# Order of the MLA up-projection and the stick-breaking value projection in a hybrid decoder trunk

## The chip, the cores and the metric

The kernel runs on one core of one Trainium2 chip. The metric is the device time of one execution in microseconds. Before the change the median of three runs is 1052.58 us, from 1045.85 to 1053.77 us.

A core has engines that run side by side, each with an instruction queue of its own: TensorE (PE in the profile; PEld is its weight load), VectorE (DVE), ScalarE (ACT), GpSimd (POOL), and SyncE (SP), which here issues transfers. An engine takes its queue in order. The order of a queue is laid down when the kernel is compiled: the order in which the Python code emits instructions is a priority, and an instruction that the compiler takes to be ready may be put ahead of one emitted earlier that is not.

## The reference, cut to what matters

Two layers; each is half a SwiGLU block, a mixing block, and half a SwiGLU block, on 256 tokens of width 1024, in float32. In the mixing block one projection `h @ w_in` feeds three groups of heads:

```python
(c_q, c_kv, k_rope, n_q, n_kc, n_vc, n_ks, n_vs, n_kw, n_vw, n_gate,
 sb_q, sb_k, sb_v) = jnp.split(h @ w_in[l], split_at, axis=-1)
o_mla = mla_attention(c_q, c_kv, k_rope, ...)       # 6 heads; q and k/v come from low-rank latents
o_nsa = nsa_attention(...)                          # 6 heads, sparse
o_sb = stick_breaking_attention(sb_q, sb_k, sb_v)   # 4 heads, no softmax
x = x + concat([o_mla, o_nsa, o_sb]) @ w_out[l]
```

MLA (latent attention) normalises the latents `c_q` (256 wide) and `c_kv` (128 wide), multiplies them by up-projections `w_uq` and `w_ukv`, and turns 32 columns of each query and of the shared key by a rotary position (rope).

## The kernel before, in words

**Matmuls.** To keep float32 accuracy each matrix is split into a high and a low part (`split`, lines 91 to 98: ACT writes the high part `wh`, DVE subtracts to get the low part `wl`), and each product takes three matmuls. Weights arrive in `raw` tiles (4 buffers); `wh` and `wl` have 5 buffers each, so a weight piece can be split only when the matmuls of an older piece are done. PSUM tiles are banks by tag (`a0`, `a1`, `g0`, `g1`), two of each.

**The mixing block** is `mix` (line 825). It projects K, Q, V and gates of the sparse heads, then the latents (`C_A`), then queries and keys of stick-breaking (`C_SQ`), then its values (`C_SV`). `project` (line 389) issues two loads of `w_in` on SP, makes four split pieces, and gives 48 matmuls on two `a0` banks, which `evac` copies out. `weave` puts steps of the sparse attention (`nsa`) between the steps of a projection, as priorities. The sparse attention has 23 steps: 5 are taken with the `C_V` projection, 10 with `C_A`, and the last 8 within the first four steps of `C_SQ`, so none is left for the weaves behind.

**The steps that the change concerns.** `latents` (line 530, called at 908) transposes the latents on PE (line 537, six transposes on `g0` and `g1`) and writes `ch` on ACT (541) and `cl` on DVE (542). The `C_SV` projection (909) and its evacuation to `SV` follow, half on ACT, half on DVE. Then `up_project` (545, called at 916) loads `w_uq` and `w_ukv` on SP (547, 550), makes three split pieces (two 576 wide, one 768 wide), and for each of two token tiles gives 18 matmuls on `g0` and `g1` (12 for the queries, 288 wide, and 6 for keys and values, 384 wide), evacuates them to `qm`, `km`, `vm`, and turns the rope columns with six POOL instructions (`rope`, lines 467 to 473: two products and a sum for the queries, the same for the key).

Then come the dense attentions: `stick_breaking` (576) transposes `SQ` (583), copies it to `sT`, and needs `SV` only for its outputs (620); `latent_attention` (625) first transposes `qm` and `km` on PE (632). Both are mixed with `out_sparse` (954), the part of the output projection that needs only the sparse heads; it takes two `a0` banks and split pieces of `w_out`.

Of the kernel before, what the change touches and what calls it, by code (L numbers as in the profile page):

```python
# [10 lines left out]
F32 = mybir.dt.float32  # L11
# [51 lines left out]
def trunk(ctx, tc, a, out):  # L63
# [4 lines left out]
    sb = ctx.enter_context(tc.tile_pool(name="sb", bufs=1))  # L68
# [5 lines left out]
    def raw_tile():  # L74
        return sb.tile([128, 2048], F32, name="raw", tag="raw", bufs=4)
# [6 lines left out]
    def bank(tag):  # L82
        return ps.tile([128, 512], F32, name="bk" + tag, tag=tag, bufs=2)
# [4 lines left out]
    def mm(o, l, r, start, stop):  # L88
        PE.matmul(o, l, r, start=start, stop=stop, skip_group_check=True)  # L89

    def split(src, n, shape=None, **dims):
        h, lo = split_tiles(n)
        hv, lv = h, lo
        if shape:
            hv, lv = h.rearrange(shape, **dims), lo.rearrange(shape, **dims)
        ACT.activation(hv, src, AF.Copy)  # L96
        DVE.tensor_tensor(lv, src, hv.bitcast(F32), op=OP.subtract)  # L97
        return hv, lv
# [75 lines left out]
    def gam(n, l, k):  # L174
        if n == "ffn1_norm":
            return cols1[:, l * KD + k:l * KD + k + 1]
        c = gcol[n, l] + k
        return cols[:, c:c + 1]
# [210 lines left out]
    def project(l, c0, c1, tag):  # L389

        w = c1 - c0
        p = [bank(tag) for _ in range(2)]

        def step(kh, k2, raw):
            W = split(raw[:, 2 * k2:2 * k2 + 2], 2 * w, "p (k f) -> p k f", k=2)
            for j in range(2):
                k = kh * 4 + k2 * 2 + j
                for t in range(2):
                    s = slice(t * 128, t * 128 + 128)
                    o = p[t][:, :w]  # L400
                    mm(o, xh[:, k, s], W[0][:, j], k == 0, False)
                    mm(o, xh[:, k, s], W[1][:, j], False, False)
                    mm(o, xl[:, k, s], W[0][:, j], False, k == KD - 1)

        for kh in range(2):
            raw = raw_tile()[:, :4 * w].rearrange("p (k f) -> p k f", k=4)
            nc.sync.dma_start(raw, a["w_in"][l, kh * 512:(kh + 1) * 512, c0:c1].rearrange("(k p) f -> p k f", p=128))
            for k2 in range(2):
                step(kh, k2, raw)
                yield p  # L410
        yield p

    def run(g, n=100):
        last = None
        for _ in range(n):
            try:
                last = next(g)
            except StopIteration:
                break
        return last  # L420

    def weave(g, h, n):

        last = None
        for last in g:
            run(h, n)
        return last

    def chain(*gens):
        for g in gens:  # L430
            yield from g
# [13 lines left out]
    def evac(i, o, p, scale):  # L445
        if i % 2 == 0:
            ACT.activation(o, p, AF.Copy, scale=scale)
        else:
            DVE.tensor_scalar(o, p, scale, None, op0=OP.mult)
# [11 lines left out]
    def rope(x, cos, sin, half, n, o=None, no=None):  # L461
        v = x.rearrange("p h (two f) -> p h two f", two=2)
        t1 = sb.tile([128, 192], F32, name="rt1", tag="rt1", bufs=2)[:, :n * 2 * half].rearrange("p (h f) -> p h f", h=n)
        t2 = sb.tile([128, 192], F32, name="rt2", tag="rt2", bufs=2)[:, :n * 2 * half].rearrange("p (h f) -> p h f", h=n)
        c = cos.rearrange("p (o f) -> p o f", o=1).to_broadcast([128, n, 2 * half])
        s = sin.rearrange("p (o two f) -> p o two f", o=1, two=2).to_broadcast([128, n, 2, half])
        POOL.tensor_tensor(t1, x, c, op=OP.mult)  # L467
        POOL.tensor_tensor(t2.rearrange("p h (two f) -> p h two f", two=2), v[:, :, ::-1, :], s, op=OP.mult)  # L468
        if o is None:
            POOL.tensor_tensor(x, t1, t2, op=OP.add)  # L470
        else:
            b = [128, no, 2 * half]
            POOL.tensor_tensor(o, t1.to_broadcast(b), t2.to_broadcast(b), op=OP.add)
# [56 lines left out]
    def latents(l, A, ch, cl):  # L530

        for b0, nb in ((0, 2), (2, 1)):
            p = bank("g%d" % (b0 // 2))
            for b in range(nb):
                for t in range(2):
                    c = (b0 + b) * 128
                    PE.transpose(p[:, b * T + t * 128:b * T + t * 128 + 128], A[:, t, c:c + 128], ident)
            for b in range(nb):
                g = gam("mla_q_norm", l, b) if b0 == 0 else gam("mla_kv_norm", l, 0)
                pb = p[:, b * T:b * T + T]  # L540
                ACT.activation(ch[b0 + b], pb, AF.Copy, scale=g)
                DVE.scalar_tensor_tensor(cl[b0 + b], pb, g, ch[b0 + b].bitcast(F32), op0=OP.mult, op1=OP.subtract)
            yield

    def up_project(l, A, ch, cl, lr, qm, km, vm):
        raw = raw_tile()[:, :1152].rearrange("p (k f) -> p k f", k=2)
        nc.sync.dma_start(raw, a["mla_w_uq"][l].rearrange("(k p) f -> p k f", p=128))
        wuq = [split(raw[:, k], 576) for k in range(2)]
        raw = raw_tile()[:, :768]
        nc.sync.dma_start(raw, a["mla_w_ukv"][l])  # L550
        wkv = split(raw, 768)
        for t in range(2):
            s = slice(t * 128, t * 128 + 128)
            q, k = qm[t], km[t]
            for c in range(2):
                p = bank("g%d" % c)[:, :288]
                f = slice(c * 288, c * 288 + 288)
                for kk in range(2):
                    mm(p, ch[kk][:, s], wuq[kk][0][:, f], kk == 0, False)
                    mm(p, ch[kk][:, s], wuq[kk][1][:, f], False, False)  # L560
                    mm(p, cl[kk][:, s], wuq[kk][0][:, f], False, kk == 1)
                evac(c, q[:, 3 * c:3 * c + 3].rearrange("p h d -> p (h d)"), p, lr[:, t:t + 1])
            for c in range(2):
                p = bank("g%d" % c)[:, :384]
                f = slice(c * 384, c * 384 + 384)
                mm(p, ch[2][:, s], wkv[0][:, f], True, False)
                mm(p, ch[2][:, s], wkv[1][:, f], False, False)
                mm(p, cl[2][:, s], wkv[0][:, f], False, True)
                ph = p.rearrange("p (h d) -> p h d", h=3)
                evac(c, k[:, 3 * c:3 * c + 3, 0:64], ph[:, :, 0:64], lr[:, 2 + t:3 + t])  # L570
                evac(c, vm[:, t, 3 * c:3 * c + 3], ph[:, :, 64:128], lr[:, 2 + t:3 + t])
            rope(q[:, :, 64:96], cosm[:, t], sinm[:, t], 16, 6)
            rope(A[:, t:t + 1, 384:416], cosm[:, t], sinm[:, t], 16, 1, o=k[:, :, 64:96], no=6)
            yield
# [250 lines left out]
    def mix(l):  # L825
# [57 lines left out]
        nsa = chain(cmp, sparse_rows(), sparse_attention(NQ, nT, gt, vbd, pct))  # L883
# [3 lines left out]
        A = sb.tile([128, 2, 448], F32, name="A", tag="A")[:, :, :416]  # L887
# [7 lines left out]
        lr = small.tile([128, 4], F32, name="lr", tag="lr")  # L895
# [6 lines left out]
        ch, cl = [chl[0][:, 0], chl[0][:, 1], chl[2][:, 0]], [chl[1][:, 0], chl[1][:, 1], chl[2][:, 1]]  # L902
        p = weave(project(l, C_SQ, C_SV, "a0"), nsa, 2)
        SQ = sb.tile([128, 2, 512], F32, name="SQ", tag="pj")
        for t in range(2):
            evac(0, SQ[:, t, 0:256], p[t][:, 0:256], r8[:, t:t + 1])
            evac(1, SQ[:, t, 256:512], p[t][:, 256:512], r[:, t:t + 1])
        run(latents(l, A, ch, cl))
        p = weave(project(l, C_SV, C_END, "a0"), nsa, 2)
        SV = sb.tile([128, 2, 256], F32, name="SV", tag="SV")  # L910
        for t in range(2):
            evac(t, SV[:, t], p[t][:, :256], r[:, t:t + 1])
        qm = [sb.tile([128, 6, 96], F32, name="qm", tag="qm", bufs=2) for _ in range(2)]
        km = [sb.tile([128, 6, 96], F32, name="km", tag="km", bufs=2) for _ in range(2)]
        vm = sb.tile([128, 2, 6, 64], F32, name="vm", tag="vm")
        weave(up_project(l, A, ch, cl, lr, qm, km, vm), nsa, 2)
        run(nsa)
        attn = mixed(stick_breaking(SQ, SV), latent_attention(qm, km, vm))

# [105 lines left out]
    for l in range(DEPTH):  # L1025
        ffn("ffn1", l, nxt=("mix_norm", l), first=l == 0)
        mix(l)
        if l + 1 < DEPTH:
            ffn("ffn2", l, nxt=("ffn1_norm", l + 1))
        else:  # L1030
            ffn("ffn2", l, final=True)
# [25 lines left out]
```

## Time and profile before

| | us |
|---|---|
| median of 3 runs | 1052.58 (1045.85 to 1053.77) |
| the profiled execution, its own time | 1054.14 |
| its span, first to last instruction | 1052.3 |
| PE busy | 1027.7 (98%) |
| DVE busy | 699.7 (66%) |
| ACT busy | 578.1 (55%) |
| POOL busy | 76.9 (7%) |

Times in a trace are microseconds from the start of the span. Busy is time in which an engine executes; it says nothing about speed. PEclk, the granted clock, is the share of full speed at which PE was let run in a stretch: 1.00 is 2.4 GHz and 0.50 is 1.2 GHz, and values between are a mean over both. The chain that ended last goes back from the last instruction, at each step to what released it. The mixing block of layer 0 ends near 344 us, that of layer 1 near 859 us.

### The profile page before, as it was taken

What the parts mean: (1) busy time and instruction counts of PE and PEld (TensorE: products, weight loads), DVE (VectorE), ACT (ScalarE), POOL (GpSimd) and SP (SyncE); (2) the same over time, 40 slices, a digit from 0 to 9 for tenths busy, and PEclk for the clock granted to TensorE, in tenths of its full rate; (3) what the DMA queues carried; (4) which work ended last, traced back from release to release, by engine and by line L of the source; (5) the groups of instructions that cost most, each with busy time, mean ns of one, the idle gap of its engine ahead of it and who ended that gap; (6) DMA issues with size and microseconds to landing.
All of it is one profiled execution on the core that took longest, in us unless ns stands there. A gap on an engine that the chain in (4) does not pass through costs nothing.

```text
span 1052.3 us, 15114 instructions
## 1 busy us (share of the span) xinstructions
PE 1027.7 (98%) x5743; PEld 874.0 (83%) x5743; DVE 699.7 (66%) x1132; ACT 578.1 (55%) x1082; POOL 76.9 (7%) x137
## 2 busy tenths in 40 slices
PE   7999999999999999999999999999999999999996
PEld 6888888897776888888888888889877778888885
DVE  6766666766635766666676666667766567666664
ACT  5555555646546655555565555556455575555553
POOL 2000000123301000000000000002142100000001
PEclk9999999999979999999999999999999999999999
DMA  9556464571322546464546556455514334645531
GB/s 314 203 181 224 140 236 152 168 233 48 117 94 81 187 174 220 143 237 165 196 136 225 178 182 216 146 200 175 190 51 130 121 121 160 238 151 211 192 129 40
DMA packets 128405, 176.38 MB, mean 168 GB/s; under 512 B 4567, under 2 KB 107213, under 8 KB 128333
## 3 DMA queue, kind: packets, MB, share of 16 engines
q1 hardware_dynamic: 127840, 174.83, 49.0%
q8 instruction: 45, 0.74, 0.3%
q10 hardware_dynamic: 492, 0.59, 0.2%
q14 instruction: 28, 0.22, 0.1%
HBM read 174.36 MB, written 1.05 MB: 167 GB/s over the span
## 4 chain that ended last, share of the span: by engine, by line
PE 90%; DVE 3%; ACT 2%; DMA 2%; POOL 2%; issue 1%; SPq 0%; POOLq 0%; ACTq 0%
PE bkg L308 45%; PE bka L89 37%; PE bkg L89 5%; DVE wl L97 1%; DMA raw<-in_ffn_w_gate_dram 1%; PE bkg L632 1%; POOL rt L467 1%; PE bkg L202 1%; ACT wh L96 0%; POOL rt L468 0%; ACT junk L213 0%; DMA x_tok<-in_x_dram 0%; DMA raw<-in_ffn_w_up_dram 0%; ACT xhl L207 0%; DMA raw<-in_w_out_dram 0%
## 5 line engine op out<-in xcount | busy, mean ns | idle before, releaser
L97 DVE TENSOR_TENSOR wl<-raw,wh 128x1024 fp32r<-128x1024 f32 (+5 forms) x336 | 395.9, 1181 | 203.9 <-ACT wh L96 201.3
L96 ACT ACTIVATE wh<-raw 128x1024 fp32r<-128x1024 f32 (+5 forms) x336 | 340.3, 1016 | 229.4 <-PE bkg L308 174.8
L308 PE MATMUL bkg<-xhl,wh 128*128 128x512 f32 (+1 forms) x1440 | 348.9, 384 | 0.2 <-DVE xhl L208 0.2
L308 PEld LDWEIGHTS bkg<-xhl,wh 128*128 128x128 f32 x1440 | 259.3, 189 | 47.9 <-PE bkg L202 0.3
L308 PEld LDWEIGHTS bkg<-xhl,wl 128*128 128x128 f32 x1392 | 189.9, 190 | 13.1
L308 PE MATMUL bkg<-xhl,wl 128*128 128x256 f32 x1392 | 195.2, 282 | 0.0
L89 PE MATMUL bka<-wh,hh 128*128 128x512 f32 x352 | 138.8, 394 | 0.3 <-ACT hh L336 0.2
L89 PE MATMUL bka<-wl,hh 128*128 128x512 f32 x352 | 138.3, 393 | 0.0
L89 PE MATMUL bka<-wh,hl 128*128 128x512 f32 x352 | 136.7, 390 | 0.6 <-DVE hl L337 0.6
L336 ACT ACTIVATE hh<-t 128x256 fp32r<-128x256 f32 x88 | 36.8, 418 | 127.0 <-DVE t L333 127.0
L89 PE MATMUL bka<-wh,xhl 128*128 128x384 f32 (+4 forms) x384 | 106.4, 349 | 0.0
L89 PEld LDWEIGHTS bka<-wh,hl 128*128 128x128 f32 x352 | 66.1, 188 | 15.8 <-DVE hl L337 1.7
L89 PEld LDWEIGHTS bka<-wh,hh 128*128 128x128 f32 x352 | 66.4, 189 | 13.2 <-ACT hh L336 2.1
L89 PEld LDWEIGHTS bka<-wl,hh 128*128 128x128 f32 x352 | 66.4, 189 | 10.3
L89 PEld LDWEIGHTS bka<-wh,xhl 128*128 128x128 f32 x384 | 68.8, 189 | 5.7 <-issue 1.7
L89 PE MATMUL bka<-wl,xhl 128*128 128x384 f32 (+4 forms) x192 | 65.9, 343 | 0.0
L337 DVE TENSOR_TENSOR hl<-t,hh 128x256 fp32r<-128x256 f32 x88 | 37.4, 425 | 40.7 <-ACT hh L336 40.7
L222 POOL TENSOR_TENSOR r<-r,nhalf 128x2 f32<-128x2 f32 x5 | 3.5, 704 | 597.8 <-DVE r L221 597.8
L459 ACT ACTIVATE P<-bka,st 128x256 f32<-128x256 f32 (+1 forms) x72 | 29.4, 418 | 22.4 <-DVE st L763 14.2
L325 DVE TENSOR_TENSOR t<-bkg,t 128x256 f32<-128x256 f32 x88 | 36.8, 418 | 6.3 <-ACT t L324 6.3
L333 DVE TENSOR_TENSOR t<-t,t 128x256 f32<-128x256 f32 x88 | 37.4, 425 | 3.8 <-ACT t L327 0.9
L326 DVE TENSOR_TENSOR t<-t,rb 128x256 f32<-128x256 f32 x88 | 37.4, 425 | 2.8
(229 smaller groups left out, 949.4 us busy)
## 6 DMA issues: line engine op xcount, KB each, us to landing
raw<-in_ffn_w_down_dram SPq DMA_DIRECT2D x44, 1024.0 KB, 6.6
raw<-in_ffn_w_gate_dram SPq DMA_DIRECT2D x43, 1024.0 KB, 6.7
raw<-in_ffn_w_up_dram SPq DMA_DIRECT2D x43, 1024.0 KB, 5.2
raw<-in_w_in_dram SPq DMA_DIRECT2D x8, 768.0 KB, 4.8
raw<-in_w_out_dram SPq DMA_DIRECT2D x20, 256.0 KB, 4.6
raw<-in_w_in_dram SPq DMA_DIRECT2D x4, 1024.0 KB, 7.1
raw<-in_w_in_dram SPq DMA_DIRECT2D x4, 832.0 KB, 4.5
raw<-in_w_in_dram SPq DMA_DIRECT2D x4, 804.0 KB, 4.4
```

The costliest lines, as they stand in the source:

```text
L89: PE.matmul(o, l, r, start=start, stop=stop, skip_group_check=True)
L96: ACT.activation(hv, src, AF.Copy)
L97: DVE.tensor_tensor(lv, src, hv.bitcast(F32), op=OP.subtract)
L202: PE.transpose(p[:, i * T + t * 128:i * T + t * 128 + 128], x_tok[:, t, d * 128:d * 128 + 128], ident)
L308: PE.matmul(*args, **flags)
L325: DVE.tensor_tensor(gn, pg[:, :T], g2, op=OP.add)
L326: DVE.tensor_tensor(gn, gn, rb, op=OP.mult)
L333: DVE.tensor_tensor(h, gn, un, op=OP.mult)
L336: ACT.activation(hh, h, AF.Copy)
L337: DVE.tensor_tensor(hl, h, hh.bitcast(F32), op=OP.subtract)
L459: state["last_exp"] = ACT.activation(*args, **kw).ins
L467: POOL.tensor_tensor(t1, x, c, op=OP.mult)
```

## The change

The latents stay where they are in the code. The whole of `up_project` (its two loads, three split pieces, 36 matmuls, evacuations and ropes) is emitted ahead of the `C_SV` projection (its two loads, four split pieces, 48 matmuls and two evacuations) instead of behind it, in both layers. No instruction is added or removed.

```diff
@@ -906,14 +906,14 @@
         run(latents(l, A, ch, cl))
-        p = weave(project(l, C_SV, C_END, "a0"), nsa, 2)
-        SV = sb.tile([128, 2, 256], F32, name="SV", tag="SV")
-        for t in range(2):
-            evac(t, SV[:, t], p[t][:, :256], r[:, t:t + 1])
         qm = [sb.tile([128, 6, 96], F32, name="qm", tag="qm", bufs=2) for _ in range(2)]
         km = [sb.tile([128, 6, 96], F32, name="km", tag="km", bufs=2) for _ in range(2)]
         vm = sb.tile([128, 2, 6, 64], F32, name="vm", tag="vm")
         weave(up_project(l, A, ch, cl, lr, qm, km, vm), nsa, 2)
+        p = weave(project(l, C_SV, C_END, "a0"), nsa, 2)
+        SV = sb.tile([128, 2, 256], F32, name="SV", tag="SV")
+        for t in range(2):
+            evac(t, SV[:, t], p[t][:, :256], r[:, t:t + 1])
         run(nsa)
         attn = mixed(stick_breaking(SQ, SV), latent_attention(qm, km, vm))
```

## Rows read from the trace of the kernel before

**Rows 1.** The page, part 4: the chain that ended last, by engine.

```profile
PE 90%; DVE 3%; ACT 2%; DMA 2%; POOL 2%; issue 1%; SPq 0%; POOLq 0%; ACTq 0%
```

**Rows 2.** Tile qm, who waited for it: us, times (both layers).

```profile
  PEld bkg L632: 4.4, 2
  PE bkg L632: 3.9, 2
```

**Rows 3.** Chain that ended last, layer 0: start, length, what.

```profile
281.72 0.44 DVE qm L449
...
284.94 1.59 POOL rt L467
286.53 0.56 POOL rt L468
287.09 0.66 POOL rt L467
287.75 1.19 POOL rt L468
288.94 0.56 POOL qm L470
289.50 0.04 issue
289.54 1.20 PE bkg L632 x7
...
344.45 0.44 PE bkg L202 x2
```

**Rows 4.** Windows: stretch, length, busy (instructions) PE, PEld, DVE, ACT, POOL; PEclk, DMA, GB/s.

```profile
284.90:290.00 5.10, 3.17 (x21) 2.37 (x19) 4.54 (x6) 2.56 (x5) 5.10 (x7) 1.00 0.36 117
290.00:344.40 54.40, 52.71 (x251) 39.14 (x249) 26.38 (x48) 29.49 (x70) 4.13 (x7) 0.87 0.26 83
344.40:500.00 155.60, 155.55 (x847) 135.20 (x848) 107.90 (x157) 85.89 (x140) 0.71 (x1) 1.00 0.55 191
```

**Rows 5.** Windows of 4 us, same columns, both layers.

```profile
288.00:292.00 4.00, 2.46 (x13) 1.77 (x13) 2.12 (x3) 0.58 (x1) 2.04 (x3) 0.80 0.47 135
292.00:296.00 4.00, 4.00 (x11) 2.86 (x10) 0.00 (x0) 1.54 (x3) 0.00 (x0) 0.50 0.00 0
...
300.00:304.00 4.00, 4.00 (x13) 3.34 (x12) 0.68 (x2) 1.91 (x5) 0.61 (x1) 0.50 0.00 0
304.00:308.00 4.00, 4.00 (x25) 3.13 (x24) 3.66 (x7) 1.55 (x2) 0.00 (x0) 0.99 0.07 10
808.00:812.00 4.00, 2.89 (x13) 2.31 (x13) 1.69 (x3) 0.58 (x1) 1.60 (x3) 0.65 0.78 242
812.00:816.00 4.00, 4.00 (x19) 3.00 (x18) 1.48 (x3) 2.23 (x6) 0.00 (x0) 0.92 0.06 23
```

**Rows 6.** Chain that ended last, layer 1: the same two places.

```profile
809.11 1.67 PE bkg L632 x7
...
859.16 0.44 PE bkg L202 x2
```

**Rows 7.** Timeline, layer 0: start, length, engine, line, out<-in; idle before.

```profile
273.99 0.55 PE L537 MATMUL bkg<-ident,A 128*128 128x128 f32 x3
274.38 0.83 ACT L541 ACTIVATE ch<-bkg,cols 128x256 fp32r<-128x256 f32 x2
275.91 0.48 DVE L542 SCALAR_TENSOR_TENSOR ch<-bkg,cols,ch 128x256 fp32r<-128x256 f32 x1 [0.15 <-ACT ch L541]
279.53 0.28 PE L89 MATMUL bka<-wh,xhl 128*128 128x256 f32 x1
279.65 0.30 PE L89 MATMUL bkg<-wh,ch 128*128 128x288 f32 x1
282.30 0.60 POOL L467 TENSOR_TENSOR rt<-qm,tab 128x192 f32<-128x192 f32 x1 [13.10 <-DVE qm L449]
284.82 1.26 DVE L97 TENSOR_TENSOR wl<-raw,wh 128x1024 fp32r<-128x1024 f32 x1 [0.22 <-ACT wh L96]
284.92 0.39 PE L89 MATMUL bka<-wh,oh 128*128 128x512 f32 x1
286.31 1.19 PE L583 MATMUL bkg<-ident,SQ 128*128 128x128 f32 x8
```

More of the change, by code (lines that the diff above doesn't have):

```diff
@@ L908, in mix @@
         run(latents(l, A, ch, cl))
+        qm = [sb.tile([128, 6, 96], F32, name="qm", tag="qm", bufs=2) for _ in range(2)]
+        km = [sb.tile([128, 6, 96], F32, name="km", tag="km", bufs=2) for _ in range(2)]
+        vm = sb.tile([128, 2, 6, 64], F32, name="vm", tag="vm")
+        weave(up_project(l, A, ch, cl, lr, qm, km, vm), nsa, 2)
         p = weave(project(l, C_SV, C_END, "a0"), nsa, 2)
@@ L912, in mix @@
             evac(t, SV[:, t], p[t][:, :256], r[:, t:t + 1])
[L913 to L916, printed above, removed]
         run(nsa)
```

## The prediction

> **What bounds the kernel now.** I read the page first. The chain that ended last is PE for 90% of the span [rows 1], so a change pays only where PE stands still or runs slowly. The changed stage lies at the end of the projections in each mixing block, and I looked there for what ends last. The tile view of the rotated queries names it: PE waits for `qm` twice, 3.9 us in all, so 1.93 us in each layer [rows 2]. The chain shows the reason: from 281.72 it leaves PE for DVE's evacuation of `qm` and POOL's ropes, and comes back at 289.54 with the transposes of line 632 [rows 3]. In the stretch from 284.90 to 290.00 PE is busy 3.17 of 5.10 us, idle for 1.93 [rows 4]. Behind it PE is busy for all but 1.69 of 54.40 us, and in the feed-forward block that follows for all but 0.05 of 155.60 us [rows 4]. So time won here is kept: nothing later in the layer stands waiting for something other than PE's own work.
>
> The second cost is one that busy time hides. The windows of 4 us show the granted clock at 1.00 before the wait; then it is at 0.50. Counted by (1 - PEclk) x 2 x 4 us, PE is at 1.2 GHz in layer 0 for 1.6 us of the window at 288, three whole windows of 4 us to 304, and 0.08 us of the next, 13.68 us in all; in layer 1 for 2.80 and 0.64 us, 3.44 us in all [rows 5]. In both layers the wait of 1.93 us is what PE did just before the clock fell. What such a microsecond costs can be read by comparing the layers, which do the same work there: from the transposes after the wait to the first transpose of the next norm, layer 0 takes 344.45 - 289.54 = 54.91 us and layer 1 859.16 - 809.11 = 50.05 us [rows 3, 6]. That is 4.86 us for 10.24 us more of half clock, 0.47 us for each; half the work is lost, and nearly all of it arrives at the end. I take 0.5.
>
> **The change, part by part.**
>
> *PE.* No matmul is added. Between the last latent transpose (it starts in the row at 273.99, and value matmuls run on from 274.3) and the first `out_sparse` matmul at 284.92, PE runs 44 value matmuls (the first four of the 48 ran earlier) and then the 36 of the up-projection without a gap [rows 7]. Both together still take 10.6 us, in whatever order. Price: 0.
>
> *The ropes.* In before, the up-projection starts at 279.65 [rows 7], and the queries of the second token tile leave POOL at 288.94 + 0.56 = 289.50 [rows 3], so 9.85 us later. In after it may start when `ch` and `cl` are there: the first two `ch` come from 274.38 on, and the last `cl` ends at 275.91 + 0.48 = 276.39 [rows 7]. With a start between 274.8 and 276.4, the queries are ready between 284.65 and 286.25. PE asks for them after its 10.6 us, the six `out_sparse` matmuls and eight `SQ` transposes, which end where the transposes of line 632 start, at about 287.2 (the row at 286.31 is 1.19 us long, the last ends modelled a little late) [rows 7]. So the ropes are done 1.0 to 2.5 us before they are wanted, and the wait goes: -1.93 x 2 = -3.86 us. The cover is the value projection; without it (all 48 value matmuls put ahead again) the 1.93 us are back.
>
> *Which order PE gets.* Emission is only a priority, so value matmuls may still fill PE while `ch` and `cl` are made. Five split buffers bound this: three up-projection pieces now come first, so two of the four value pieces fit beside them. At most 24 of 48 value matmuls can run early, and at least 24 x 0.12 us = 2.9 us remain (44 took 279.65 - 274.3 = 5.35 us) behind the up-projection. That is more than the 1.93 us which is to be covered.
>
> *Loads and splits.* Both sets of loads were done long before, and each takes the other's place on SP; the three up-projection pieces are split while the stick-breaking query projection runs, where two value pieces were split. I cost this at 0: PE covers it, and with the cover gone it is one split, 1.26 us at its longest [rows 7].
>
> *What is late next.* `SV` is now evacuated last, and `out_sparse` wants the same two `a0` banks. Its first matmul can be held by an evacuation that is itself queued behind one DVE split (1.26 us, [rows 7]) and takes about 0.48 us, the length of the neighbouring DVE row. PE has about 0.9 us of `SQ` transposes for the meantime [rows 7]. Bounds: 0 to 0.8 us in a layer. I take 0.3, nearer the lower end since the compiler may put the transposes first: +0.6. `stick_breaking` itself needs `SV` only after its scores, so nothing else queues on it.
>
> *The clock.* If PE no longer stands still there, the half-clock stretches go too: (13.68 + 3.44) x 0.5 = 8.56 us. The lower bound for this part is 0, the stretches staying for another reason; the upper is 8.56. I take 8.56, as the only long idle stretch ahead of both falls is the one that goes.
>
> **Sum**, against the profiled execution's own time: 1054.14 - 3.86 - 8.56 + 0.6 = 1042.3 us. That execution lies 1.56 us above the median of the runs shown, and the fastest of them, at 1045.85, lies 8.3 us below it: about what an execution without either half-clock stretch would show, though no row says so.
>
> A rule of the Trainium skill that speaks against the change is in "SBUF — State Buffer", section "Who interferes with whom": a VectorE instruction with two inputs in SBUF and a GpSimd instruction that reads SBUF exclude each other. This case's trace agrees: the rope of 192 columns takes 0.60 us at 282.30 and 1.59 us at 284.94, when a split of 1.26 us runs on DVE [rows 3, 7]. By that rule the value splits now fall among the ropes and lengthen them: the sum would be that of rival C, where the first tile's row alone gives that of A.
>
> **Rivals.**
>
> *A, the forecast.* Wait and half clock both gone: 1042.3 us, with 2.5 us to either side for the new bank wait and a different mixture of the attention behind.
>
> *B, the wait goes, a half-clock stretch stays in one layer.* For it: the two stretches differ fourfold in length after the same idle [rows 5], so something other than that idle decides how long they are. Time 1042.3 + 1.7 = 1044.0 with the short one, 1042.3 + 6.8 = 1049.1 with the long one.
>
> *C, the change doesn't do what it says: the ropes stay late.* Either PE's queue gets most values first after all, or the first tile's ropes are stretched as the second's are. The first tile's six instructions take 2.64 us, from 282.30 to 284.94; the second tile's first five take 4.56 us, to 289.50 [rows 3, 7]. Stretched alike, the first tile adds 1.92 us and puts the queries at up to 286.25 + 1.92 = 288.17, 1.0 us after PE wants them. Against it: that needs the latest start and both tiles beside DVE's splits. Time: with values first, 1054; with a wait of 1.0 for 1.93 in each layer and the half clock kept, 1054.14 - 1.86 = 1052.3; with the shorter half-clock stretch in both layers 5.1 less, 1047.2.
>
> *D, slower.* The compiler puts the up-projection's matmuls into PE's queue with no value matmul before them, and PE stands in front of `cl`: 276.39 - 274.3 = 2.1 us in each layer [rows 7], in place of the 1.93. A half-clock stretch begins there, where all 80 matmuls are dense. With a long stretch in both layers the time is 1054.14 + (13.68 - 3.44) x 0.5 + 0.3 = 1059.6. It is slower by over 1% only if the stretches pass 17 us in each layer. Against it: two value pieces are split by then, and the trace fills such places with value matmuls already.
>
> *E, better.* With attention starting 2 us earlier against the DVE splits, the 1.69 us of idle that are left in each layer [rows 4] go as well: 1042.3 - 3.4 = 1038.9.
>
> **How the numbers follow.** Chances: A 0.58, B 0.15, C 0.13, D 0.05, E 0.09. The likeliest gives 1042.3 us, with its own range 1039.8 to 1044.8. The range for 8 in 10 reaches from E's neighbourhood to the middle of C: 1038.0 to 1052.0; it leaves out D, half of C and a little of E. A measurement of this kernel can tell about 1% from no change; 1% under the median is 1042.05, which cuts A in two. Faster by over 1%: half of A and E, 0.38. Within 1%: the rest of A, B, C and most of D, 0.58. Slower by over 1%: 0.04, D with very long stretches and what I don't see.
>
> **What would show it.** In the profile after, the first `bkg<-wh,ch` matmul should start within about 2 us of the last latent transpose, with at least 24 value matmuls behind the last of the up-projection; the wait of line 632 for POOL should be under 0.3 us; PEclk should stand at 1.00 through both mixing blocks; and the first `out_sparse` matmul may show a wait for `SV`. Wrong would be: PE idle in front of the up-projection, a wait for `qm` that is still over 1 us, or a granted clock of 0.50 with no idle ahead of it. The last would take away 8.6 of the 11.8 us that I forecast.

## The result, and the profile after

The changed kernel takes 1043.03 us (median of four runs, 1042.12 to 1044.06), the kernel before 1052.28 beside it (four runs, 1045.85 to 1053.77): a ratio of 0.9923, with a 95% interval from 0.9894 to 0.9952. That is within 1%, though the interval reaches a little past it. The forecast was 1042.3. The profiled execution of after took 1044.06 us of its own time with a span of 1042.3; before's took 1054.14 with 1052.3. Some runs of before are much nearer: its fastest is 1045.85. The four runs of after lie within 1.9 us, the four of before within 7.9.

The wait that the forecast started from is gone. These are the waits of PE in after, from 268 to 345 us, then those from 780 to 860 us (what PE waited for; us in total, times, longest):

```profile
PE bka L89 <- DVE SV L449: 1.0, 1, 1.0
PE bkg L89 <- DVE PT L455: 0.5, 1, 0.5
PE bkg L202 <- DVE x_tok L952: 0.2, 1, 0.2
```

Both layers give the same three lines. The one for POOL's `qm` [rows 2] is missing, and a new one stands at the top: `out_sparse` waits 1.0 us for `SV`. In before the same view reads, in either layer:

```profile
PE bkg L632 <- POOL qm L470: 1.9, 1, 1.9
PE bka L89 <- ACT P L459: 1.0, 1, 1.0
...
```

The two lines below are those of after. Here a second line has gone that nobody moved: 1.0 us for `P`, the exponentials of an attention's scores. It is part of the 1.69 us of idle that the prediction counted behind the stage [rows 4].

The timeline of after, layer 0, shows the new order (start, length, engine, line, out<-in; idle before):

```profile
275.30 0.66 PE L537 MATMUL bkg<-ident,A 128*128 128x128 f32 x4
...
276.31 0.40 PE L89 MATMUL bkg<-wh,ch 128*128 128x288 f32 x1
...
281.72 0.33 PE L89 MATMUL bkg<-wh,ch 128*128 128x384 f32 x1
281.89 0.28 PE L89 MATMUL bka<-wh,xhl 128*128 128x256 f32 x1
281.90 1.06 POOL L467 TENSOR_TENSOR rt<-qm,tab 128x192 f32<-128x192 f32 x1
...
283.07 5.41 DVE L97 TENSOR_TENSOR wl<-raw,wh 128x512 fp32r<-128x512 f32 x5
...
285.35 1.04 POOL L470 TENSOR_TENSOR qm<-rt,rt 128x192 f32<-128x192 f32 x1
...
286.40 0.47 ACT L447 ACTIVATE SV<-bka,r 128x256 f32<-128x256 f32 x1 [0.45 <-PE bka L89]
286.44 0.28 PE L89 MATMUL bka<-wh,xhl 128*128 128x256 f32 x1
...
288.40 0.47 DVE L449 TENSOR_SCALAR SV<-bka,r 128x256 f32<-128x256 f32 x1
288.93 0.50 PE L89 MATMUL bka<-wh,oh 128*128 128x512 f32 x1 [1.04 <-DVE SV L449]
...
289.74 0.81 PE L583 MATMUL bkg<-ident,SQ 128*128 128x128 f32 x6
...
290.39 0.60 PE L632 MATMUL bkg<-ident,qm 128*96 128x128 f32 x4
```

The up-projection (`bkg<-wh,ch`) begins 1.0 us after the last latent transposes and ends near 282. From 281.89 to 286.72 PE runs 39 value matmuls (counted over all rows between the two that stand here). The ropes' last query result leaves POOL at 286.39, and PE comes for it at 290.39.

The row at 283.07 merges a run of five splits, of 512 and 1,024 columns, under the form of its first one. It is the new trouble. PE ends the value matmuls at 286.72; ACT had already copied one half of `SV`, but DVE's half stands in its queue behind these splits until 288.40, and the fourth `out_sparse` matmul (288.93) needs that half's bank. Six of the eight `SQ` transposes (289.74) stand behind that matmul in PE's queue and so can't fill the wait.

The windows compare the whole mixing block, from the first transpose of its norm to the first of the next norm (stretch, length, busy (instructions) PE, PEld, DVE, ACT, POOL; PEclk, DMA, GB/s). Before, layers 0 and 1:

```profile
195.64:344.45 148.81, 144.57 (x880) 117.84 (x878) 92.31 (x187) 84.78 (x206) 32.32 (x56) 0.95 0.36 117
715.27:859.16 143.89, 139.61 (x881) 114.39 (x878) 92.25 (x187) 84.49 (x206) 32.45 (x56) 0.99 0.39 124
```

After, layers 0 and 1:

```profile
197.02:337.62 140.60, 138.18 (x881) 113.01 (x878) 92.12 (x187) 84.85 (x206) 33.33 (x56) 1.00 0.38 124
708.48:849.11 140.63, 138.21 (x880) 113.03 (x878) 92.07 (x187) 84.86 (x206) 33.44 (x56) 1.00 0.39 127
```

Length less PE's busy time is PE's idle time: 4.24 and 4.28 us before, 2.42 and 2.42 after. Busy time fell as well, by 6.39 and 1.40 us, with the same matmuls at a granted clock of 1.00 instead of 0.95 and 0.99. So the two blocks are together 3.68 us shorter by less idle and 7.79 us by a faster clock: 11.47 us. Outside the blocks the two executions differ in one place. After's ran at half clock near its start, where before's did not:

```profile
24.00:28.00 4.00, 3.38 (x10) 2.48 (x10) 3.47 (x7) 2.45 (x7) 0.00 (x0) 0.66 0.83 297
28.00:32.00 4.00, 4.00 (x21) 3.46 (x20) 2.40 (x4) 3.14 (x4) 0.00 (x0) 0.91 0.04 15
```

Its first block starts 1.38 us later for that (197.02 against 195.64). 11.47 - 1.38 = 10.09, and the two own times differ by 1054.14 - 1044.06 = 10.08. Just before it PE had waited 1.12 us for a tile of the feed-forward block, where before's wait is 0.22. The change itself doesn't reach the start: a second profiled execution of after, below, has 1.00 there.

### The profile page after: what moved, and what is told of

Its sections match the earlier page's. It is cut to its first block, busy times and chain, and to the rows that moved or that the text cites. A ratio compares the mean times of both kernels' runs of the same rounds, so it can differ in the third digit from the quotient of the medians.

```text
span 1042.3 us, 15114 instructions
## 1 busy us (share of the span) xinstructions
PE 1019.9 (98%) x5743; PEld 867.1 (83%) x5743; DVE 699.4 (67%) x1132; ACT 578.6 (56%) x1082; POOL 78.9 (8%) x137
## 4 chain that ended last, share of the span: by engine, by line
PE 93%; DVE 3%; ACT 2%; issue 1%; DMA 1%; POOL 0%; POOLq 0%; SPq 0%; DVEq 0%; ACTq 0%
PE bkg L308 46%; PE bka L89 37%; PE bkg L89 6%; DVE wl L97 1%; PE bkg L632 1%; PE bkg L202 1%; ACT junk L213 0%; ACT wh L96 0%; DMA x_tok<-in_x_dram 0%; DMA raw<-in_ffn_w_up_dram 0%; ACT xhl L207 0%; PE bkg L782 0%; PE bkg L106 0%; DVE x_tok L263 0%; POOL wl L1018 0%
```

## The experiments

**Is it PE's idle time that brings the half clock?** The kernel before, with 16 matmuls put into PE's queue ahead of the transposes of line 632. Their result is used by nothing; the order of the projections stays.

```diff
-            qk = []
+            qk = []; [mm(f, xh[:, k % KD, 0:128], xh[:, k % KD], k == 0, k == 15)
+                      for f in [bank("a1")[:, :T]] * (pr == 0) for k in range(16)]
```

> The kernel before, with 16 matmuls of 128x256 (about 1.9 us) put on TensorE in each layer between the SQ transposes and the first qm transposes, where it stood idle for 1.93 us; their result is not used. My theory: the idle draws the clock down. With the idle filled the wait is still paid (by the added work), but the granted clock stays at 1.00: 1052.3 - 8.6 = about 1044, at most 1047. Rival 1 (the clock falls for what comes there anyway: short transposes, the slow start of the attention): a stretch at 0.50 stays, 1051 to 1054. Rival 2 (the gain needs the value projection behind the up-projection): also 1051 to 1054, with the clock at 1.00.

1045.23 us (10 runs, 1043.23 to 1045.92); ratio 0.995, interval 0.993 to 0.997. PE has more work and the kernel is faster. The windows of this kernel behind the place of the wait, and its whole blocks:

```profile
288.00:292.00 4.00, 3.96 (x31) 3.31 (x31) 2.76 (x4) 1.10 (x2) 3.05 (x5) 1.00 0.43 124
292.00:296.00 4.00, 4.00 (x23) 3.12 (x22) 2.01 (x5) 3.04 (x9) 0.21 (x1) 1.00 0.04 13
...
196.68:337.84 141.16, 139.79 (x895) 114.79 (x894) 91.97 (x187) 84.72 (x206) 31.83 (x56) 1.00 0.38 123
708.71:850.11 141.40, 139.79 (x895) 114.83 (x893) 92.19 (x187) 84.67 (x206) 31.99 (x56) 1.00 0.39 126
```

The clock stays at 1.00 where it was 0.80 and 0.50 [rows 5], with no change to the projections' order. The mean granted clock of a whole execution, recorded for every run, agrees: 0.996 to 0.998 in all ten, and 0.993 or less in 12 of the 20 runs of before beside them. So filling the 1.93 us is enough. The wait for `P` is gone in this kernel too, so its gain is not the clock's alone: of 7.65 us in layer 0 (148.81 - 141.16), idle is 2.87 and busy time 4.78, after the 16 matmuls have been paid.

**The reverse: the new order, with the ropes made late.** The kernel after, with eight further products on POOL ahead of the second token tile's ropes; their results are unused.

```diff
+            [POOL.tensor_tensor(z, q[:, :, 64:96], q[:, :, 64:96], op=OP.mult)
+             for z in [tmp(3)[:, :192].rearrange("p (h d) -> p h d", h=6)] * t for _ in range(8)]
             rope(q[:, :, 64:96], cosm[:, t], sinm[:, t], 16, 6)
```

> The kernel after, with eight added POOL products of 128x192 (0.6 us each alone, up to 1.2 beside splits) ahead of the second token tile's ropes in each layer, their result not used, so that qm is late again. TensorE's order stays that of after but for a few mask matmuls. My theory: the wait of the line 632 transposes for POOL comes back with 1.5 to 4 us in each layer, and the clock falls to 0.50 behind it for 3 to 14 us in each layer: 1043 + 3 to 8 + 3.5 to 13.7, so 1050 to 1064. Rival (the clock has its fall from elsewhere and the idle costs only itself): 1046 to 1051 with the clock at 1.00 in the mixing blocks.

1060.02 us (4 runs, 1057.46 to 1060.72); ratio 1.01, interval 1.0069 to 1.0132. The waits of PE in layer 0, and the windows of 4 us in layer 1:

```profile
PE bkg L632 <- POOL qm L470: 2.9, 1, 2.9
PE bka L89 <- DVE SV L449: 1.1, 1, 1.1
...
808.00:812.00 4.00, 1.14 (x9) 0.86 (x7) 0.72 (x2) 0.58 (x1) 3.05 (x6) 0.88 0.76 236
812.00:816.00 4.00, 4.00 (x15) 2.96 (x14) 0.69 (x1) 1.57 (x3) 0.00 (x0) 0.50 0.06 26
...
820.00:824.00 4.00, 4.00 (x12) 3.24 (x13) 0.78 (x3) 2.90 (x9) 0.61 (x1) 0.50 0.00 0
824.00:828.00 4.00, 4.00 (x24) 3.23 (x24) 2.90 (x6) 2.04 (x3) 0.00 (x0) 0.92 0.72 208
```

The half clock comes back with the wait: 13.6 us of it here, 6.9 us in layer 0. Against after the blocks are longer by 146.86 - 140.60 = 6.26 and 149.88 - 140.63 = 9.25 us. The 2.9 us of wait leave 3.4 and 6.4 for the clock, 0.49 and 0.47 us for each half-clock microsecond. The wait for `P` does not come back, though the ropes are later than in before. So that wait belongs to the order laid down for PE's queue behind the stage and not to the moment at which attention starts.

**Is the new wait for `SV` DVE's queue?** The kernel after, with both halves of `SV` copied by ACT.

```diff
-            evac(t, SV[:, t], p[t][:, :256], r[:, t:t + 1])
+            evac(0, SV[:, t], p[t][:, :256], r[:, t:t + 1])
```

> The kernel after, with both halves of SV evacuated on ACT instead of one on DVE. My theory: the new wait of 1.04 us in each layer is the DVE half of SV standing behind splits on DVE; with ACT free there the wait falls under 0.3 us and the time by 1.5 to 2.1 us, to 1041 to 1041.5. Rival (the bank wait only uncovers the next one, the transposes' copies or POOL): the wait goes but the time stays at 1043 within 0.5.

1041.64 us (5 runs, 1039.9 to 1043.63); ratio 0.9923, interval 0.9894 to 0.9951. PE's wait for `SV` is gone. The difference to after is about the spread of the runs, so this kernel was timed again beside after, on the same chip:

> The kernel after with both halves of SV evacuated on ACT, again, to set it against the kernel after on one chip. My theory: 1.5 to 2.1 us under after_b. Rival (the wait that went was hidden by something else): the same as after_b within 0.5 us.

> The kernel after, again, beside the two others on one chip: 1042 to 1044, the clock at 1.00 in both mixing blocks.

1040.68 us (4 runs, 1039.87 to 1041.34) against 1043.05 for after (4 runs, 1041.59 to 1044.06); their runs don't overlap. The ratios to before (1051.53, 13 runs) are 0.99, interval 0.9865 to 0.9935, and 0.9919, interval 0.9888 to 0.995. Of this kernel, the two copies and the fourth `out_sparse` matmul in the timeline, which has no idle ahead of it, then its layer 0 block:

```profile
284.61 0.84 ACT L447 ACTIVATE SV<-bka,r 128x256 f32<-128x256 f32 x2 [0.45 <-PE bka L89]
...
285.93 0.40 PE L89 MATMUL bka<-wh,oh 128*128 128x512 f32 x1
...
195.21:334.60 139.39, 138.00 (x880) 113.18 (x878) 91.41 (x186) 85.33 (x207) 33.48 (x56) 1.00 0.38 125
```

Idle in the block falls from 2.42 to 1.39 us, by the 1.04 us of the wait. Two layers give 2.1 us, and the medians differ by 2.4, a little more than was expected. This is a version that beats both kernels. The second execution of after has blocks of 140.59 and 140.57 us and 1.00 at the start; its own time is 1042.29.

**Can the ropes be made early without moving the projections?** The kernel before, with the key's ropes, which need nothing of the up-projection, put right behind the latents' projection. POOL then has three instructions less in each token tile.

```diff
+        for t in range(2):
+            rope(A[:, t:t + 1, 384:416], cosm[:, t], sinm[:, t], 16, 1, o=km[t][:, :, 64:96], no=6)
         ...
-            rope(A[:, t:t + 1, 384:416], cosm[:, t], sinm[:, t], 16, 1, o=k[:, :, 64:96], no=6)
```

> The kernel before, with the shared key's ropes (six POOL instructions of line 473's helper call for both token tiles) emitted right behind the latents' projection, when POOL is free, instead of between the queries' ropes. The value projection stays ahead of the up-projection. My theory: it is only the late qm that cost time; POOL's chain gets about 2.4 us shorter, the wait of 1.93 us goes, and the clock stays at 1.00: 1040 to 1043.5, the same gain as the reordering. Rival (the reordering itself, the value matmuls behind the up-projection, is what gains): 1050 to 1053. If the wait shrinks to under 1 us and the clock still falls, 1046 to 1050.

1044.12 us (10 runs, 1043.45 to 1047.25); ratio 0.9954, interval 0.9933 to 0.9975. That is 0.6 us above the range that was expected. Its waits of PE in layer 0:

```profile
PE bka L89 <- ACT P L459: 1.0, 1, 1.0
PE bkg L89 <- DVE PT L455: 0.5, 1, 0.5
PE bkg L582 <- DVE vm L449: 0.3, 1, 0.3
PE bkg L89 <- DVE sT L455: 0.2, 1, 0.2
```

Neither `qm` nor `SV` is in the list; the clock is 1.00 in both blocks. This edit removes the wait and keeps the clock up as the changed order does. It keeps the wait for `P`, and with small new ones its idle is 3.17 us in a block against 2.42 in after. The queries are ready at 288.15 (POOL's last row there is at 287.55 and 0.60 us long) and PE comes at 288.28, so this route has 0.1 us to spare where after has 4.0.

**Loads and splits alone.** The kernel before, with the loads and the split pieces of the up-projection ahead of the value projection and its matmuls still behind.

```diff
+        up = up_project(l, A, ch, cl, lr, qm, km, vm)
+        next(up)                      # loads and splits, up to a new yield
         p = weave(project(l, C_SV, C_END, "a0"), nsa, 2)
         ...
-        weave(up_project(l, A, ch, cl, lr, qm, km, vm), nsa, 2)
+        weave(up, nsa, 2)
```

> One part of the change alone: the loads and the three split pieces of the up-projection come ahead of the value projection, its 36 matmuls stay behind all 48 value matmuls. My theory: weights were never late, so nothing is gained; the wait for qm stays at about 1.9 us in each layer and half-clock stretches follow it: 1050 to 1054 (to 1047 if the stretch in layer 0 is short). Rival (the earlier weights, or the other order of loads and splits, is what gains): under 1046.

1052.59 us (10 runs, 1048.29 to 1057.59); ratio 1.0011, interval 0.9988 to 1.0035. PE still waits 1.9 us for `qm` in each layer. So what the change gains, it gains by the order of the matmuls and not by that of the loads and splits. In its profiled execution (1049.71 us) each layer has 3.4 us at half clock, from windows of 0.70 and 0.87 in layer 0 and of 0.63 and 0.94 in layer 1.

**What makes a half-clock stretch long?** The kernel before again, one more profiled execution.

> The kernel before, profiled once more. Its times of the last series fall into two groups, about 1045.4 to 1048.6 and 1050.9 to 1054.1. My theory: the groups differ in how long the granted clock stays at 0.50 behind the wait for qm; at a time near 1046 to 1048 the stretches would be about 3.4 us in each layer, near 1052 to 1054 about 14 us in one. Rival (the groups differ elsewhere, as in the first 30 us): the stretches are the same as in the first profile whatever the time is.

1051.31 us. Both waits of 1.9 us are there. The windows behind them, layer 0 and layer 1:

```profile
288.00:292.00 4.00, 2.24 (x13) 1.54 (x13) 2.34 (x3) 0.58 (x1) 2.26 (x3) 0.88 0.48 135
292.00:296.00 4.00, 4.00 (x11) 3.08 (x11) 0.16 (x1) 1.53 (x3) 0.00 (x0) 0.50 0.00 0
296.00:300.00 4.00, 4.00 (x12) 3.02 (x11) 1.61 (x5) 2.75 (x11) 0.61 (x1) 0.50 0.01 2
300.00:304.00 4.00, 4.00 (x20) 3.32 (x19) 1.62 (x4) 2.53 (x5) 0.61 (x1) 0.84 0.00 0
804.00:808.00 4.00, 2.07 (x15) 1.48 (x14) 3.69 (x6) 1.73 (x3) 4.00 (x6) 1.00 0.26 87
808.00:812.00 4.00, 4.00 (x25) 3.10 (x23) 0.94 (x2) 1.84 (x4) 0.30 (x1) 1.00 0.60 189
```

In layer 0 this is 10.2 us at half clock, in layer 1 none. Another 3.4 us stand near the start (0.90 and 0.68 in the windows from 8 to 16 us). The same wait in the same kernel gave 13.7 and 3.4 us in the first execution [rows 5]. The expectation, about 14 us in one layer at such a time, was not met as it stood. The length differs from execution to execution, and nothing that was run says by what.

**Fewer POOL instructions beside the splits.** The kernel after, with the early key ropes of the edit above; and the same with both `SV` halves on ACT as well.

> The kernel after, with the shared key's ropes emitted right behind the latents' projection as in e4_key_early; SV is evacuated on DVE and ACT as in after. In the trace of after five splits of 512 columns on DVE take 5.41 us, 1.08 us each, where one takes 0.69 us when POOL is free, and SV stands behind them. My theory: part of the bank wait of 1.04 us is POOL and DVE holding each other up; with the key's three POOL instructions of the second tile gone from there (3.5 us) the five splits take 4.5 us or less, the wait of out_sparse for SV falls under 0.4 us, and the time by 1.2 to 2.1 us, to 1041 to 1041.8. Rival (the splits follow ACT and the buffers, not POOL): the five splits and the wait stay, 1043.

> The kernel after with SV evacuated on ACT and the key's ropes early, both together. My theory: each alone takes the same wait of 1.04 us away, so together they give no more than one: 1040 to 1041.7. Rival (they are worth something each): under 1039.5.

1042.27 us (4 runs, 1041.33 to 1042.92; ratio 0.9919, interval 0.9887 to 0.9952) and 1040.29 us (5 runs, 1039.97 to 1042.12; 0.9902, interval 0.9869 to 0.9934). The first misses its expected range by 0.5 us, the second lies in it. In the first, DVE's run of five splits and PE's wait behind it:

```profile
281.50 4.87 DVE L97 TENSOR_TENSOR wl<-raw,wh 128x512 fp32r<-128x512 f32 x5
...
PE bka L89 <- DVE SV L449: 0.2, 1, 0.2
```

The splits take 4.87 us for 5.41 (4.5 or less was expected), so POOL's ropes had slowed DVE as DVE slowed them, and the wait falls from 1.0 to 0.2. The block falls only from 140.59 to 140.24 us. One reason is in the trace: a wait of the sparse attention (ahead of a transpose at 248.44 in this kernel) is 0.73 us with the early ropes and 0.39 in after, so idle in the block falls by 0.53 us (2.42 to 1.89) and not by 0.84. The kernels with `SV` on ACT differ in the same way, 0.7 against 0.4. By which step the early ropes lengthen it was not followed up. With `SV` on ACT as well, the early ropes bring nothing: 139.82 us in a block against 139.39 without them. The block is no longer held by the ropes or by `SV` there.

## Why the prediction was right, step by step

**The wait for `qm`, -3.86 us: right.** The view that found it [rows 2, 3] has no such line after, in either layer. The queries were due between 284.65 and 286.25; they came at 286.39 in an execution that was 1.38 us late at that point, so at 285.0 in the terms of the forecast. They are 4.0 us early for PE, where 1.0 to 2.5 was forecast. Part of the difference is the `SV` wait (1.04 us), which holds PE back too.

**The order that PE gets: right.** At least 24 value matmuls were to remain behind the up-projection as cover; 39 do.

**The ropes beside the splits.** Rival C's contention is real: the first product of the second token tile takes 1.06 us and the sum for `qm` 1.04, where 0.60 is what such a row takes alone [rows 7]. The stretched rows all run beside splits; this agrees with the rule of the Trainium skill cited in the prediction ("SBUF — State Buffer", "Who interferes with whom"). The contention did not decide, since PE comes 4.0 us later and all the stretching fits in there. Rival C took PE to come at 287.2.

**The new wait for a bank, +0.6 us: the step that failed.** It measured 1.04 us in each layer, 2.08 in all, above the upper bound of 0.8. The prediction put *one* split ahead of DVE's half of `SV`. In the trace it is a run of five, 5.41 us long, and DVE is in the fourth of them when PE ends its matmuls at 286.72. Taken one by one the five are 512, 1,024, 512, 1,024 and 512 columns wide. The value projection has four pieces of 512, and three of them were split earlier (the last at 281.49), so only the first of the five is a piece that moved. The other four belong to the output projection, which stayed where it was. In before DVE copied its half of `SV` between the first two of these, with the others behind (one of them at 284.82 [rows 7]):

```profile
279.50 1.23 DVE L97 TENSOR_TENSOR wl<-raw,wh 128x1024 fp32r<-128x1024 f32 x1 [0.69 <-ACT wh L96]
280.65 0.48 DVE L449 TENSOR_SCALAR SV<-bka,r 128x256 f32<-128x256 f32 x1
281.04 0.68 DVE L97 TENSOR_TENSOR wl<-raw,wh 128x512 fp32r<-128x512 f32 x1
```

So the copy moved in among splits that had followed it, and the bound of one split was too low. The cover that the prediction counted on is mostly missing too: six of the eight `SQ` transposes stand behind the waiting matmul. Giving that copy to ACT removes the wait, and 2.4 us of time.

**The clock, -8.56 us: right in kind, a little large.** Both half-clock stretches are gone, and PE's busy time fell by 6.39 + 1.40 = 7.79 us for 17.12 us at half clock, 0.46 us for each. The two layers of before, read alone, had said 0.47; rounding it up to 0.5 is about half of the 0.8 us that the term is too large. The filled kernel shows that the idle of 1.93 us brings the half clock, and the late-rope kernel that an idle of 2.9 us brings it in the new order as well. It does not always follow: one of the four layer passes of before that were profiled had none behind the same idle. After's new idle of 1.04 us brought none in any of the four layer passes that were profiled. Rival B is out for these executions; of the other runs of after only the mean clock is known, 0.995 to 0.997.

**What lies behind, 0 forecast: -2.0 us.** Rival E held that the 1.69 us of idle in each layer could go as well. 1.0 us of it did, though not for E's reason, the earlier start of attention: a matmul of the output projection no longer waits for the bank that `P` is read from. It is the 43rd of the projection's 96 matmuls in the layer. `out_sparse` gives 36 of these, so it belongs to `out_late`, the part that needs the dense heads, whose second half takes the `a1` banks of the latent attention's scores. In before that row is:

```profile
326.14 0.47 ACT L459 ACTIVATE P<-bka,st 128x256 f32<-128x256 f32 x1 [3.05 <-DVE st L498]
...
327.22 0.50 PE L89 MATMUL bka<-wh,oh 128*128 128x512 f32 x1 [1.00 <-ACT P L459]
```

In after, PE's queue has two of the projection's matmuls on another bank (319.58, 319.89) at that point:

```profile
318.78 1.04 PE L89 MATMUL bkg<-t,mats 128*128 128x256 f32 x6
319.58 0.47 PE L89 MATMUL bka<-wl,oh 128*128 128x512 f32 x1
319.89 0.40 PE L89 MATMUL bka<-wh,ol 128*128 128x512 f32 x1
320.40 0.50 PE L89 MATMUL bka<-wh,oh 128*128 128x512 f32 x1
```

They fill the time until ACT has read the bank. The order is the compiler's and was not part of the edit. The late-rope kernel keeps it while its ropes come late, and the filled kernel has it too, though its projections stand as in before. What makes the compiler choose it was not tried.

**The sum.** -3.86 + 2.08 - 2.00 - 7.79 = -11.57, against 11.47 measured in the blocks; the prediction had -11.82. The total agrees to 0.4 us by luck: two misses of 1.5 and 2.0 us, and one of 0.8, nearly cancel. The `P` term in particular was not foreseen. The median of after, 1043.03, is 0.7 us above the forecast and inside the likeliest case's own range. Half clock at the start, which the forecast does not hold, cost 1.38 us in one profiled execution of after and nothing in the other.

The gain against the *median* of before rests on how long its half-clock stretches are. Before's runs go from 1045.41 to 1054.09 us over 20 runs in one series. An execution without half clock in its blocks would take about 1054.14 - 7.79 = 1046.4. None was profiled, but the recorded mean clock of each run bears this out. Of the 41 runs of before timed beside the experiments, the eight at 0.998 took 1045.41 to 1046.72 us (median 1046.1), and the 24 at 0.991 or less took 1050.07 to 1054.51. The one run of after at 0.998 took 1042.29. Between runs at this clock the change is worth 3.8 us, close to the 3.68 us of idle; the rest of its gain over the median goes with the half clock that before has and after mostly hasn't.

## What to carry to other kernels

Read the granted clock behind every idle stretch of TensorE: here two idle stretches of 1.93 us cost 3.9 us themselves and, in the profiled execution, 7.8 us of busy time behind them, and 16 unused matmuls put into each gap brought the time down from 1051.8 to 1045.2 us (the wait for `P`, 1.0 us in each layer, went there as well). Whoever moves a stage gets its last evacuation at a new place: look at the whole queue of the engine that makes it, not at one row, and give it to the engine that is free. When what is late needs only part of its inputs (the key's ropes), starting that part early can be worth as much as moving a whole stage.

## What was not expected of the hardware

After the same idle of 1.93 us, one kernel showed 0, 3.4, 10.2 and 13.7 us of half clock in four layer passes of two executions, and this sets most of the spread of its runs. Why the length differs stays open.

Shorter idle can be followed by it too. Between the two layers' mixing blocks PE waits 0.37 and then 1.00 us, 1.4 us apart, in all twelve profiled executions. In three of them 3.4 us at half clock follow (0.74 and 0.83 in the windows from 524 to 532 us of the kernel before with early key ropes, where 520 to 524 has 1.00), and in the other nine none. So an idle of 1.0 us is not safe everywhere, though after's was.

VectorE and GpSimd slow each other: a GpSimd product of 192 columns goes from 0.60 to as much as 1.59 us beside splits [rows 3, 7], and five splits go from 4.87 to 5.41 us when five rope instructions run beside them rather than two.
